# Gate and up of SwiGLU as seven block products for eight, in parts of 8, 8 and 6 tiles

## Chip, core and metric

One Trainium2 chip, one of its cores. The metric is the device time of one execution in microseconds: the median of three runs. All data are float32.

## What is computed

A trunk of four layers on 512 tokens of width 1024. Each layer has a mixer (stick-breaking attention, gMLP, Mamba-2, attention again) and then a SwiGLU FFN with 2816 hidden columns. The change is in the FFN alone:

```python
def swiglu(h, w_gu, w_down):
    gu = h @ w_gu                     # (512, 1024) @ (1024, 5632)
    return (jax.nn.silu(gu[..., :FFN_HIDDEN]) * gu[..., FFN_HIDDEN:]) @ w_down

x = x + swiglu(rmsnorm(x, ffn_norm[i]), ffn_w_gu[i], ffn_w_down[i])
```

## The kernel before

**Layout.** Activations lie transposed: eight tiles `xT[d]` of 128 features by 512 tokens. A float32 product is made from three products of split operands: each operand is a high part (`hi`, a cast to the rounded type fp32r) and a low part (`lo`, the rest), and `mm3` (L420) issues hi*hi, hi*lo and lo*hi. The normed input is kept as `xh[d]` and `xl[d]`, with the norm's gain in it but without the norm's row factor; that factor, `rstdB`, is multiplied in after the product. `xl` is made by a weighted subtraction on VectorE (L570).

**Weights.** `Stream` (L263) brings weights in the order of their use. A piece of 1 MB (1024 x 256 columns) lands in a `raw` tile, of which there are two, by DMAs of SyncE's queue. `_split` (L321) makes the high part on ScalarE or VectorE (`to_hi`, L433 and L435) and the low part on VectorE or GpSimd (`to_lo`, by `either`, L454 and L456), half a piece at a time, 128 x 1024, into rings of three `whi` and three `wlo` tiles.

**The FFN.** `ffn` runs in two parts of 12 and 10 hidden tiles (a tile is 128 columns). For each pair of tiles `fm` (L677) makes gate, then up: two PSUM banks, eight k tiles, 3 matmuls of 512 columns each, 48 matmuls with a piece. A gate's bank is multiplied by `rstdB` (L785), goes through Silu on ScalarE (L788) and once more by `rstdB`; an up's bank is multiplied by that (L802), and the result is split into `hi` and `lo` for the down projection. After a part, `outp` runs its share of the down projection and adds it to `xT` (`residual`, L600). The next sublayer's `xh` and `xl` are made as the last part's residuals come.

**What sets the order.** `Order` (L72) is a planner that runs while the kernel is recorded: it books each operation on its engine with a cost, spawns the chains that follow a matmul, and lets a matmul be recorded when the planned time of what it needs has come. `either`, `to_hi` and `from_psum` choose the engine that is free first in that plan. What it records is the fixed order of each engine's queue; on the chip each queue runs in that order and waits where it must.

## Time and profile before

| what | value |
|---|---|
| median of three runs | 2842.22 us (2841.31 to 2843.84) |
| the profiled execution, its time | 2840.29 us |
| the profiled execution, its span | 2838.6 us |
| TensorE (PE) busy | 2773.0 us, 98% |
| VectorE (DVE) busy | 1837.8 us, 65% |
| ScalarE (ACT) busy | 940.2 us, 33% |
| GpSimd (POOL) busy | 499.5 us, 18% |
| mean granted TensorE clock | 0.993 |

The four FFN stages lie at about 335 to 680, 985 to 1340, 1810 to 2160 and 2480 to 2838 us. PE's matmuls overlap in the trace, since their ends are modelled; the pace of a stream of matmuls is read from its starts. PEld are PE's loads of the stationary operand.

### The profile page before, as it was taken

Reading aid. Unit: us, or ns where it says so; the run is one execution under the profiler, and the core shown is the slowest. Engines: PE = TensorE matmul, PEld = TensorE weight load, DVE = VectorE, ACT = ScalarE, POOL = GpSimd, SP = SyncE. Lnnn points to the kernel's source line nnn. Section 1 sums busy time; section 2 is a strip of 40 time slices with the busy share of each in tenths; the row PEclk is TensorE's granted clock in tenths of the full one; section 3 lists DMA queues with packets and bytes.
Section 4 is the critical chain, followed back from the end, with each engine's and each line's share of the span. In section 5 each row is a group of like instructions: output and inputs, shape, how many; then the busy total and the mean of one; then the engine's idle time right before and its main releaser. Section 6 shows DMA issues by size and latency. Waiting matters only on the chain.

```text
span 2838.6 us, 35548 instructions
## 1 busy us (share of the span) xinstructions
PE 2773.0 (98%) x14531; PEld 2367.4 (83%) x14531; DVE 1837.8 (65%) x2657; ACT 940.2 (33%) x1615; POOL 499.5 (18%) x424
## 2 busy tenths in 40 slices
PE   8999899999999999999999999999999999899999
PEld 8988688888988888888898898788888988688887
DVE  7898754455465655454887797754545899865452
ACT  4777410113322211112453353310112677511111
POOL 4555300002010100001121121100003555300000
PEclk9999999999999999999999999999999999999999
DMA  3110232323332223233222222223222111232222
GB/s 122 60 60 23 82 104 89 102 84 121 99 97 93 89 93 100 89 100 93 77 75 75 81 79 65 89 89 104 89 93 93 54 60 38 68 100 93 93 97 78
DMA packets 212644, 240.77 MB, mean 85 GB/s; under 512 B 6512, under 2 KB 179696, under 8 KB 212480
## 3 DMA queue, kind: packets, MB, share of 16 engines
q1 hardware_dynamic: 212224, 238.36, 26.4%
q8 instruction: 114, 1.87, 0.3%
q14 instruction: 50, 0.41, 0.0%
q0 software_dynamic: 160, 0.11, 0.0%
q10 hardware_dynamic: 96, 0.03, 0.0%
HBM read 236.38 MB, written 2.10 MB: 84 GB/s over the span
## 4 chain that ended last, share of the span: by engine, by line
PE 85%; DVE 12%; ACT 1%; issue 1%; POOL 0%; DMA 0%; ACTq 0%; DVEq 0%; POOLq 0%
PE ps L412 78%; PE c L412 2%; PE z L412 2%; DVE r L454 2%; DVE x L600 1%; DVE xl L570 1%; DVE s L1568 1%; DVE wlo L454 1%; DVE r L435 1%; DVE whi L435 1%; PE t L412 1%; PE c L426 1%; DVE of L1648 0%; DVE s L454 0%; DVE lo L454 0%
## 5 line engine op out<-in xcount | busy, mean ns | idle before, releaser
L412 PE MATMUL ps<-xl,whi 128*128 128x512 f32 x1792 | 700.7, 391 | 4.7 <-DVE xl L570 4.2
L412 PE MATMUL ps<-xh,whi 128*128 128x512 f32 x1792 | 704.2, 393 | 0.0
L412 PE MATMUL ps<-xh,wlo 128*128 128x512 f32 x1792 | 699.1, 390 | 0.0
L454 DVE TENSOR_TENSOR wlo<-raw,whi 128x1024 fp32r<-128x1024 f32 (+2 forms) x413 | 507.7, 1229 | 124.7 <-ACT whi L433 107.1
L433 ACT CAST whi<-raw 128x1024 fp32r<-128x1024 f32 (+2 forms) x235 | 231.0, 983 | 978.9 <-PE ps L412 941.9
L435 DVE CAST whi<-raw 128x1024 fp32r<-128x1024 f32 (+2 forms) x234 | 168.2, 719 | 399.7 <-PE ps L412 399.2
L412 PEld LDWEIGHTS ps<-xl,whi 128*128 128x128 f32 x1792 | 337.5, 188 | 79.6 <-DVE xl L570 9.4
L412 PEld LDWEIGHTS ps<-xh,whi 128*128 128x128 f32 x1792 | 337.5, 188 | 71.3 <-issue 1.4
L412 PEld LDWEIGHTS ps<-xh,wlo 128*128 128x128 f32 x1792 | 337.5, 188 | 70.6
L412 PE MATMUL ps<-hi,wlo 128*128 128x512 f32 x960 | 382.7, 399 | 0.0
L412 PE MATMUL ps<-lo,whi 128*128 128x512 f32 x960 | 379.7, 396 | 0.8 <-DVE lo L454 0.8
L412 PE MATMUL ps<-hi,whi 128*128 128x512 f32 x960 | 380.3, 396 | 0.0
L412 PE MATMUL ps<-whi,xh 128*128 128x256 f32 x1280 | 368.1, 288 | 0.0
L412 PE MATMUL ps<-wlo,xh 128*128 128x256 f32 x1280 | 363.1, 284 | 3.5 <-DVE wlo L454 3.5
L412 PE MATMUL ps<-whi,xl 128*128 128x256 f32 x1280 | 363.0, 284 | 0.0
L412 PEld LDWEIGHTS ps<-wlo,xh 128*128 128x128 f32 x1280 | 245.7, 192 | 5.6 <-DVE wlo L454 3.7
L412 PEld LDWEIGHTS ps<-whi,xh 128*128 128x128 f32 x1280 | 245.7, 192 | 2.3 <-issue 0.2
L412 PEld LDWEIGHTS ps<-whi,xl 128*128 128x128 f32 x1280 | 245.6, 192 | 0.0
L412 PEld LDWEIGHTS ps<-lo,whi 128*128 128x128 f32 x960 | 180.6, 188 | 45.6 <-DVE lo L454 1.5
L412 PEld LDWEIGHTS ps<-hi,whi 128*128 128x128 f32 x960 | 180.7, 188 | 42.3 <-ACT hi L433 0.3
L412 PEld LDWEIGHTS ps<-hi,wlo 128*128 128x128 f32 x960 | 180.8, 188 | 42.2
L456 POOL TENSOR_TENSOR lo<-a,hi 128x512 fp32r<-128x512 f32 x4 | 7.5, 1873 | 1173.8 <-DVE hi L435 1173.8
(232 smaller groups left out, 3435.0 us busy)
## 6 DMA issues: line engine op xcount, KB each, us to landing
raw<-in_ffn_w_gu SPq DMA_DIRECT2D x88, 1024.0 KB, 5.1
raw<-in_ffn_w_down SPq DMA_DIRECT2D x32, 1024.0 KB, 5.1
raw<-in_sb_w_qkv SPq DMA_DIRECT2D x23, 1024.0 KB, 5.2
raw<-in_gm_w_in SPq DMA_DIRECT2D x16, 1024.0 KB, 5.4
raw<-in_ssm_w_in SPq DMA_DIRECT2D x16, 1024.0 KB, 5.5
raw<-in_ffn_w_down SPq DMA_DIRECT2D x16, 768.0 KB, 4.4
raw<-in_gm_w_out SPq DMA_DIRECT2D x8, 1024.0 KB, 5.1
raw<-in_ssm_w_in SPq DMA_DIRECT2D x16, 512.0 KB, 5.3
```

Source lines behind the costliest of these rows:

```text
L412: self.nc.tensor.matmul(out, lhsT=lhsT, rhs=rhs, start=start, stop=stop, skip_group_check=True)
L426: self.nc.tensor.transpose(out, in_, self.ident[:in_.shape[0], :in_.shape[0]])
L433: self.nc.scalar.copy(h, src)
L435: self.nc.vector.tensor_copy(h, src)
L454: self.nc.vector.tensor_tensor(out, a, b, op=op)
L456: self.nc.gpsimd.tensor_tensor(out, a, b, op=op)
L570: nc.vector.scalar_tensor_tensor(out=self.xl[d], in0=x, scalar=gcol(d), in1=self.xh[d].bitcast(F32), op0=ALU.mult, op1=ALU.subtract)
L600: nc.vector.tensor_tensor(self.xT[d], self.xT[d], ps, op=ALU.add)
L1568: nc.vector.scalar_tensor_tensor(out=e, in0=zz, scalar=0.0, in1=e, op0=ALU.max, op1=ALU.add)
```

## The change

Gate and up pieces (all but the first pair of each FFN) go by Strassen's algorithm in Winograd's form. A piece A has 1024 rows by 256 columns, cut into 2 x 2: A11, A12, A21, A22, where the first index is the half of the 256 columns and the second is even or odd k tiles. The input B is cut likewise: even or odd feature tiles, first or second 256 tokens. A piece and the input make a *unit*. With S1 = A21 + A22, S2 = S1 - A11, S3 = A11 - A21, S4 = A12 - S2 and T1 = B12 - B11, T2 = B22 - T1, T3 = B22 - B12, T4 = B21 - T2 (B11, B12 being the token halves of the even tiles) there are seven products: A11 B11, A12 B21, S4 B22, A22 T4, S1 T1, S2 T2, S3 T3. Each is 4 k tiles x 3 matmuls of 256 columns, and the code calls it by the name of its weight factor.

- `halves_in` makes T1 to T4 once per FFN from `xT` and the gains, with differences on ScalarE, VectorE and GpSimd, and splits them into `th` and `tl` tiles of the FFN's pool. No unit starts before all are there; the plain first pair stands ahead of them.
- `_sums` makes S1 to S4 by four operations of 128 x 512 per piece. `_factor` splits each of the seven factors, 512 columns at a time, into one tile that holds high and low part: five of a piece in the `whi` and `wlo` rings (six slots), A22 and S4 in a ring `wt` of two. A third landing tile, `more`, stands beside the two `raw`.
- `fast` orders the products. Three PSUM banks hold a unit's partial sums: X takes A11, S2, S3 and A22 one upon the other, Y takes A12, Z takes S1 and S4. After A11, after S2 and after S3, X is copied out (`saved`, on ScalarE or VectorE), and the next product on X waits for that copy. `added` adds Y or Z to such a copy on VectorE. The last quarter of the result is multiplied straight from X. A unit's A22 and S4 are issued within the next unit; those of a part's last unit stand behind the first piece of the down projection (`between`).
- The parts are 8, 8 and 6 hidden tiles in place of 12 and 10, so `outp` runs three times for each FFN.

```diff
+    def add_fast(self, src):
+        raw = {"srcs": [src], "left": 7, "tag": ("more", "raw", "raw")[self.n_fast % 3], "loaded": Task(), "fast": {}}
+        self.n_fast += 1
+        self.raws.append(raw)
+        for name in ("A11", "A12", "S2", "S1", "S3", "A22", "S4"):
+            p = raw["fast"][name] = {"raw": raw, "task": Task(), "name": name, "slots": 1, "ready": Task()}
+            (self.tails if name in ("A22", "S4") else self.pieces).append(p)
+        return raw["fast"]
...
+    def _sums(self, r):
+        o, fast = self.o, r["fast"]
+        yield r["task"]
+        A = {(i, j): r["ap"][:, j - 1::2, (i - 1) * P:i * P] for i in (1, 2) for j in (1, 2)}
+        fast["A11"]["src"], fast["A12"]["src"], fast["A22"]["src"] = A[1, 1], A[1, 2], A[2, 2]
+        for name in ("A11", "A12", "A22"):
+            o.finish(fast[name]["ready"])
+        new = lambda nm: self.k.fpool.tile([P, 4, P], F32, tag=nm, name="sum", bufs=1)
+        def put(name, dst, a, b, op):
+            yield self.k.either(dst, a, b, op, 512)
+            fast[name]["src"] = dst
+            o.finish(fast[name]["ready"])
+        yield self.k.take("S1", 1)
+        s1 = new("S1")
+        yield from put("S1", s1, A[2, 1], A[2, 2], ALU.add)
+        yield self.k.take("S2", 1)
+        s2 = new("S2")
+        yield from put("S2", s2, s1, A[1, 1], ALU.subtract)
+        yield from put("S3", A[2, 1], A[1, 1], A[2, 1], ALU.subtract)
+        yield fast["A12"]["task"]
+        yield from put("S4", A[1, 2], A[1, 2], s2, ALU.subtract)
+        yield fast["S2"]["task"]
+        self.k.put("S2")
...
+    def _factor(self, p, before, placed, tail=False):
+        if not tail:
+            tag = ("whi", "wlo")[self.turn]
+            self.turn = 1 - self.turn
+        yield p["raw"]["loaded"]
+        yield [p["ready"], before]
+        if tail:
+            t = self.k.fpool.tile([P, 1024], F32R, tag="wt", name="wt", bufs=2)
+        else:
+            t = self.k.wp.tile([P, 1024], F32R, tag=tag, name=tag, bufs=WB)
+        self.o.finish(placed)
+        h, l = (t[:, c:c + 512].rearrange("p (a b) -> p a b", b=P) for c in (0, 512))
+        yield self.k.to_hi(h, p["src"], 512)
+        yield self.k.to_lo(l, p["src"], h, 512, self.slack)
+        p["h"], p["l"] = h, l
+        if p["name"] == "S1":
+            self.k.put("S1")
+        self._done(p)
...
+            b, t12, t34 = (pool.tile([P, S], F32R, tag=f"a{2 + n // 2}{'hl'[n % 2]}", name="t", bufs=1).bitcast(F32)
+                           for n in range(3 * p, 3 * p + 3))
+            T = [t12[:, :H], t12[:, H:], t34[:, :H], t34[:, H:]]
+            nc.scalar.activation(b[:, :H], x0[:, :H], AF.Copy, scale=g0)
+            yield o.A(H, ap=1)
+            stt = lambda out, x, g, y: nc.vector.scalar_tensor_tensor(out=out, in0=x, scalar=g, in1=y,
+                                                                      op0=ALU.mult, op1=ALU.subtract)
+            stt(T[0], x0[:, H:], g0, b[:, :H])
+            yield o.V(H, 1)
+            stt(T[1], x1[:, H:], g1, T[0])
+            yield o.V(H, 1)
+            e = self.either(T[2], T[1], b[:, :H], ALU.subtract, H)
+            stt(T[3], x1[:, :H], g1, T[1])
+            yield [e, o.V(H, 1)]
+            th = self.th[p] = pool.tile([P, 4, H], F32R, name=f"th{p}", bufs=1)
+            tl = self.tl[p] = pool.tile([P, 4, H], F32R, name=f"tl{p}", bufs=1)
+            for n, t in enumerate((t12, t34)):
+                h, l = (q[:, 2 * n:2 * n + 2, :].rearrange("p a b -> p (a b)") for q in (th, tl))
+                yield self.to_hi(h, t, S)
+                e = self.to_lo(l, t, h, S)
+            yield e
+            o.finish(self.t_ready[p])
...
+    def factor_x(self, name, p):
+        H = S // 2
+        if name in ("A11", "A12", "S4"):
+            k, c = {"A11": (0, 0), "A12": (1, 0), "S4": (1, H)}[name]
+            return self.xh[2 * p + k][:, c:c + H], self.xl[2 * p + k][:, c:c + H]
+        n = {"S1": 0, "S2": 1, "S3": 2, "A22": 3}[name]
+        return self.th[p][:, n, :], self.tl[p][:, n, :]
+    def product(self, u, name, bank, start):
+        p = u.p[name]
+        for k in range(4):
+            x, w = self.factor_x(name, k), (p["h"][:, k, :], p["l"][:, k, :])
+            for n, (a, b) in enumerate(((0, 0), (0, 1), (1, 0))):
+                self.nc.tensor.matmul(bank[:, :S // 2], lhsT=w[a], rhs=x[b], start=start and k == 0 and n == 0,
+                                      stop=False, skip_group_check=True)
+                self.o.pe(0.1207)
+        self.stream.release(p)
...
+        def saved(dst, ps, task):
+            if o.pick(A=0.00083 * H + 0.1, V=0.00104 * H + 0.07) == "A":
+                nc.scalar.copy(dst, ps[:, :H])
+                yield o.A(H, True)
+            else:
+                nc.vector.tensor_copy(dst, ps[:, :H])
+                yield o.V(H)
+            o.finish(task)
+        def added(dst, ps, after, task, give):
+            yield after
+            nc.vector.tensor_tensor(dst, ps[:, :H], dst, op=ALU.add)
+            yield o.V(H)
+            if give:
+                self.give()
+            o.finish(task)
+        def p4(u):
+            yield o.due(u.p["A22"]["task"], u.s3)
+            self.product(u, "A22", u.X, False)
+            o.spawn(u.quarter(u.X))
+        def p3(u):
+            yield o.due(u.p["S4"]["task"], u.c22)
+            self.product(u, "S4", u.Z, False)
+            o.spawn(added(u.t[0][:, H:], u.Z, u.s2, u.c12, True))
+        prev = None
+        for u in units:
+            u.s1, u.s2 = Task(), Task()
+            yield self.both(o.due(u.p["A11"]["task"], *self.t_ready), self.bank_cond())
+            u.X = self.bank()
+            self.product(u, "A11", u.X, True)
+            u.t = u.make()
+            o.spawn(saved(u.t[0][:, :H], u.X, u.s1))
+            yield self.both(o.due(u.p["A12"]["task"]), self.bank_cond())
+            u.Y = self.bank()
+            self.product(u, "A12", u.Y, True)
+            o.spawn(added(u.t[0][:, :H], u.Y, u.s1, u.c11, True))
+            o.spawn(u.rest())
+            if prev is not None:
+                yield from p4(prev)
+            yield o.due(u.p["S2"]["task"], u.s1)
+            self.product(u, "S2", u.X, False)
+            o.spawn(saved(u.t[0][:, H:], u.X, u.s2))
+            if prev is not None:
+                yield from p3(prev)
+            yield self.both(o.due(u.p["S1"]["task"]), self.bank_cond())
+            u.Z = self.bank()
+            self.product(u, "S1", u.Z, True)
+            yield o.due(u.p["S3"]["task"], u.s2)
+            self.product(u, "S3", u.X, False)
+            o.spawn(saved(u.t[1][:, H:], u.X, u.s3))
+            o.spawn(added(u.t[1][:, H:], u.Z, u.s3, u.c22, False))
+            prev = u
+        def tail():
+            yield from p4(prev)
+            yield from p3(prev)
+        return tail()
...
+                    yield from between
+                    between = ()
...
-        for nf in (12, 10):
+        for nf in (8, 8, 6):
...
-                gu.append([self.reg_in([wgu[:, :, b + f * P:b + (f + 2) * P]]) for b in (0, HID)])
+                cols = [wgu[:, :, b + f * P:b + (f + 2) * P] for b in (0, HID)]
+                gu.append([self.reg_in([c]) if f == 0 else self.reg_fast(c) for c in cols])
...
+                def quarter(un, by, ready):
+                    def gen(ps):
+                        yield ready
+                        nc.vector.tensor_tensor(un.t[1][:, :H], ps[:, :H], by()[:, :H], op=ALU.mult)
+                        yield o.V(H)
                         self.give()
-                        nc.scalar.activation(gates[i], gates[i], AF.Silu)
-                        yield o.A(S, tab="silu")
-                        yield self.either(gates[i], gates[i], self.rstdB, ALU.mult, S)
-
-                    tasks = {}
-
-                    def gate_(i, ps, tasks=tasks, gate=gate):
-                        tasks[i] = o.spawn(gate(i, ps))
+                        o.finish(un.c21)
+                    return gen
+                def rest(un, by, ready, then):
+                    def first():
+                        yield [un.c11, un.c12, ready[0]]
+                        yield times(un.t[0], slice(0, S), by(0))
+                        yield from then(0)
+                    def second():
+                        yield [un.c22, ready[1]]
+                        e = times(un.t[1], slice(H, S), by(1))
+                        yield [un.c21, e]
+                        yield from then(1)
...
+                def gated(i):
+                    yield from silu(g.t[i])
+                    o.finish(done[i])
+                r = self.rstdB_ready
+                g.quarter = quarter(g, lambda: self.rstdB, r)
+                g.rest = rest(g, lambda i: self.rstdB, [r, r], gated)
+                u.quarter = quarter(u, lambda: g.t[1], done[1])
+                u.rest = rest(u, lambda i: g.t[i], done, lambda i: self.parts(two[i], pool, f"a{n0 + i}", u.t[i]))
+                return [g, u]
```

On **PE**, in the kernel before, the first up block of the first FFN. `ps` is a PSUM bank, the pair behind it is the moving tile and the stationary tile:

```order
L412 MATMUL ps_3969<-xh0_80,whi_3882 128x512
L412 MATMUL ps_3969<-xl0_88,whi_3882 128x512
L412 MATMUL ps_3969<-xh0_80,wlo_3883 128x512
L412 MATMUL ps_3969<-xh1_81,whi_3882 128x512
L412 MATMUL ps_3969<-xl1_89,whi_3882 128x512
L412 MATMUL ps_3969<-xh1_81,wlo_3883 128x512
```

The changed kernel, in the second part of the same FFN: the end of product A12 into bank Y of a unit, then A22 of the unit before it into that one's bank X, and S2 into the current unit's X.

```order
L847 MATMUL ps_5293<-xh7_87,whi_5206 128x256
L847 MATMUL ps_5293<-xl7_95,whi_5206 128x256
L847 MATMUL ps_5293<-xh7_87,whi_5206 128x256
L847 MATMUL ps_5178<-th0_3982,wt_4992 128x256
L847 MATMUL ps_5178<-tl0_3983,wt_4992 128x256
L847 MATMUL ps_5178<-th0_3982,wt_4992 128x256
L847 MATMUL ps_5178<-th3_4068,wt_4992 128x256
L847 MATMUL ps_5272<-th0_3982,wlo_5224 128x256
L847 MATMUL ps_5272<-tl0_3983,wlo_5224 128x256
L847 MATMUL ps_5272<-th0_3982,wlo_5224 128x256
L847 MATMUL ps_5236<-xh1_81,wt_5130 128x256
```

Moving tiles are half as wide, and between A11 and S2 on the same bank stand the 24 matmuls of A12 and of the former unit's A22.

On **DVE**, in the kernel before, most of one gate and one up block in a steady stretch (`g` and `a` are gate and up results):

```order
L785 TENSOR_TENSOR g_4385<-ps_4330,rstdB_3995 128x512
L454 TENSOR_TENSOR g_4385<-g_4385,rstdB_3995 128x512
L785 TENSOR_TENSOR g_4403<-ps_4331,rstdB_3995 128x512
L454 TENSOR_TENSOR wlo_4407<-raw_4310,whi_4406 128x1024
L454 TENSOR_TENSOR g_4403<-g_4403,rstdB_3995 128x512
L435 CAST whi_4436<-raw_4310 128x1024
L454 TENSOR_TENSOR wlo_4437<-raw_4310,whi_4436 128x1024
L802 TENSOR_TENSOR a_4453<-ps_4400,g_4385 128x512
L435 CAST hi_4459<-a_4453 128x512
L454 TENSOR_TENSOR lo_4460<-a_4453,hi_4459 128x512
L802 TENSOR_TENSOR a_4473<-ps_4401,g_4403 128x512
L435 CAST hi_4482<-a_4473 128x512
```

The changed kernel, twelve of the 37 rows that it has for the same two blocks. L870 adds a partial result from PSUM, `sum`, and `raw` or `more` as an output, are S1 to S4, and `wlo`, `whi` and `wt` are low parts written into a factor's tile:

```order
L556 TENSOR_TENSOR sum_5504<-raw_5396 128x512
L556 TENSOR_TENSOR a_5291<-a_5291,g_5198 128x512
L556 TENSOR_TENSOR sum_5516<-sum_5504,raw_5396 128x512
L537 CAST hi_5524<-a_5291 128x512
L556 TENSOR_TENSOR wlo_5521<-more_5208,wlo_5521 128x512
L556 TENSOR_TENSOR lo_5525<-a_5291,hi_5524 128x512
L870 TENSOR_TENSOR g_5423<-ps_5495,g_5423 128x256
L556 TENSOR_TENSOR whi_5545<-raw_5396,whi_5545 128x512
L556 TENSOR_TENSOR g_5423<-g_5423,rstdB_4118 128x256
L556 TENSOR_TENSOR wlo_5566<-raw_5396,wlo_5566 128x512
L870 TENSOR_TENSOR a_5557<-ps_5559,a_5557 128x256
L556 TENSOR_TENSOR raw_5396<-raw_5396,sum_5516 128x4x128
```

Two subtractions of 1024 per piece became seven of 512 and four sums, and the additions from PSUM stand between them in the same queue.

On **DVE** at the start of the first FFN, in the kernel before, from the last residual on:

```order
L600 TENSOR_TENSOR x7_79<-x7_79,ps_3866 128x512
L570 SCALAR_TENSOR_TENSOR xl4_92<-x4_76,cols0_143,xh4_84 128x512
L570 SCALAR_TENSOR_TENSOR xl5_93<-x5_77,cols0_143,xh5_85 128x512
L454 TENSOR_TENSOR wlo_3883<-raw_3763,whi_3882 128x1024
L570 SCALAR_TENSOR_TENSOR xl6_94<-x6_78,cols0_143,xh6_86 128x512
L570 SCALAR_TENSOR_TENSOR xl7_95<-x7_79,cols0_143,xh7_87 128x512
L454 TENSOR_TENSOR acc_3820<-acc_3820,sq_3918 128x512
L454 TENSOR_TENSOR wlo_3928<-raw_3763,whi_3927 128x1024
L643 TENSOR_SCALAR ms_3960<-ps_3953 128x4
L652 TENSOR_SCALAR diag_3958<-ident_96,rstd_3876 128x128 x4
```

The changed kernel, from the last `xl` tile on (the rows go on for 14 more to the last `tl` tile):

```order
L671 SCALAR_TENSOR_TENSOR xl7_95<-x7_79,cols0_143,xh7_87 128x512
L537 CAST wt_3947<-more_3886 128x512
L813 SCALAR_TENSOR_TENSOR t_3927<-x4_76,cols0_143,t_3926 128x256
L813 SCALAR_TENSOR_TENSOR t_3883<-x1_73,cols0_143,t_3882 128x256
L556 TENSOR_TENSOR acc_3820<-acc_3820,sq_3937 128x512
L813 SCALAR_TENSOR_TENSOR t_3909<-x3_75,cols0_143,t_3909 128x256
L556 TENSOR_TENSOR sum_3973<-sum_3949,more_3886 128x512
L556 TENSOR_TENSOR wt_3947<-more_3886,wt_3947 128x512
L813 SCALAR_TENSOR_TENSOR t_3927<-x5_77,cols0_143,t_3927 128x256
L813 SCALAR_TENSOR_TENSOR t_3970<-x6_78,cols0_143,t_3969 128x256
L556 TENSOR_TENSOR acc_3820<-acc_3820,sq_3958 128x512
L813 SCALAR_TENSOR_TENSOR t_3910<-x3_75,cols0_143,t_3909 128x256
```

The differences T (L813) and first factors of the weights stand where two subtractions of weights stood.

## Rows read from the trace of the kernel before

**Rows 1.** The page's busy time (share) and instructions of each engine.

```profile
PE 2773.0 (98%) x14531; PEld 2367.4 (83%) x14531; DVE 1837.8 (65%) x2657; ACT 940.2 (33%) x1615; POOL 499.5 (18%) x424
```

**Rows 2.** Windows: stretch, length, busy PE, PEld, DVE, ACT, POOL; clock, DMA share, GB/s.

```profile
335.00:680.00 345.00, 345.00 (x1502) 282.44 (x1501) 177.92 (x220) 51.70 (x64) 8.26 (x5) 1.00 0.29 92
521.00:532.00 11.00, 11.00 (x50) 9.02 (x49) 4.52 (x6) 1.05 (x1) 0.00 (x0) 1.00 0.28 95
312.00:342.00 30.00, 25.85 (x95) 18.98 (x94) 20.32 (x27) 15.69 (x24) 11.78 (x7) 0.89 0.22 71
100.00:240.00 140.00, 133.88 (x934) 123.66 (x934) 132.40 (x208) 107.62 (x221) 84.72 (x69) 1.00 0.15 51
1460.00:1480.00 20.00, 20.00 (x143) 18.75 (x142) 19.06 (x36) 12.83 (x18) 4.89 (x4) 1.00 0.21 54
```

**Rows 3.** Timeline of PE in gate and up; start, duration, engine, line, operation.

```profile
399.84 0.39 PE L412 MATMUL ps<-xh,whi 128*128 128x512 f32 x1
...
412.53 0.39 PE L412 MATMUL ps<-xh,wlo 128*128 128x512 f32 x1
```

**Rows 4.** Timeline of PE in the first mixer, 256 columns.

```profile
173.88 0.28 PE L412 MATMUL ps<-wlo,xh 128*128 128x256 f32 x1
...
175.55 0.28 PE L412 MATMUL ps<-whi,xh 128*128 128x256 f32 x1
```

**Rows 5.** Timeline of PE in the first FFN's down projection.

```profile
479.62 0.39 PE L412 MATMUL ps<-lo,whi 128*128 128x512 f32 x1
...
483.82 0.39 PE L412 MATMUL ps<-lo,whi 128*128 128x512 f32 x1
```

**Rows 6.** Timeline of DVE behind an up block.

```profile
410.24 0.69 DVE L802 TENSOR_TENSOR a<-ps,g 128x512 f32<-128x512 f32 x1 [0.93 <-PE ps L412]
410.96 0.43 DVE L435 CAST hi<-a 128x512 fp32r<-128x512 f32 x1
411.42 0.69 DVE L454 TENSOR_TENSOR lo<-a,hi 128x512 fp32r<-128x512 f32 x1
```

**Rows 7.** Timeline of DVE in the third mixer.

```profile
1407.20 0.68 DVE L1122 TENSOR_TENSOR xp<-ps,rstdB 128x512 f32<-128x512 f32 x1
1407.80 1.21 DVE L454 TENSOR_TENSOR wlo<-raw,whi 128x1024 fp32r<-128x1024 f32 x1
1408.94 0.74 DVE L1130 SCALAR_TENSOR_TENSOR cv<-xp,cols,cv 128x512 f32<-128x512 f32 x1
1409.60 0.41 DVE L1252 TENSOR_TENSOR h<-h,c 128x256 f32<-128x256 f32 x1
1409.93 0.74 DVE L1130 SCALAR_TENSOR_TENSOR cv<-xp,cols,cv 128x512 f32<-128x512 f32 x1
```

**Rows 8.** Groups of instructions over the whole run: count, busy us, mean ns, idle before.

```profile
L435 DVE CAST whi<-raw 128x1024 fp32r<-128x1024 f32 x213 | 154.0, 723 | 397.6 <-PE ps L412 397.1
...
L435 DVE CAST hi<-a 128x512 fp32r<-128x512 f32 x88 | 37.6, 427 | 3.0
...
L454 DVE TENSOR_TENSOR wlo<-raw,whi 128x768 fp32r<-128x768 f32 x32 | 33.9, 1059 | 88.9 <-ACT whi L433 88.9
...
L1497 DVE SCALAR_TENSOR_TENSOR v<-ps,rstd,v 128x256 fp32r<-128x256 f32 x32 | 15.3, 478 | 8.3 <-ACT v L1495 7.9
...
L1246 ACT COPY h<-c 128x256 f32<-128x256 f32 x8 | 3.0, 370 | 16.7 <-PE c L412 16.7
```

**Rows 9.** The same for DVE between 100 and 240 us.

```profile
L454 DVE TENSOR_TENSOR r<-s,r 128x512 fp32r<-128x512 f32 x28 | 22.8, 816 | 0.8 <-ACT r L433 0.4
L435 DVE CAST r<-s 128x512 fp32r<-128x512 f32 x23 | 15.9, 693 | 0.5 <-ACT s L1611 0.2
...
L454 DVE TENSOR_TENSOR r<-s,r 128x256 fp32r<-128x256 f32 x14 | 9.5, 687 | 0.1
```

**Rows 10.** Timeline of DVE before the first FFN.

```profile
312.41 0.75 DVE L570 SCALAR_TENSOR_TENSOR xl<-x,cols,xh 128x512 fp32r<-128x512 f32 x1 [0.19 <-ACT xh L568]
...
314.28 1.68 DVE L570 SCALAR_TENSOR_TENSOR xl<-x,cols,xh 128x512 fp32r<-128x512 f32 x1
```

173 lines of the change are left out of this document (128 added, 45 removed).

## The prediction

> **What bounds the kernel now.** I read the busy times first [rows 1]: TensorE (PE) holds 98% of the span, VectorE (DVE) 65%, ScalarE (ACT) 33%, GpSimd (POOL) 18%. Then the stretches [rows 2]: in the first SwiGLU stage (335 to 680 us) PE is busy 345.00 of 345 us at granted clock 1.00 and DVE 177.92. A busy PE is a modelled figure, so the pace is taken from starts. In gate and up, matmuls of 512 columns start every 0.2266 us: 56 intervals between the first and the last row of [rows 3]. Nothing else is waited for there; only fewer or shorter matmuls can help, and DVE's spare half is what may be spent.
>
> **PE's share of the change.** A unit is one gate or up block: 1024 rows by 256 weight columns, against 512 tokens. It was 2 x 8 x 3 = 48 matmuls of 512 columns, 48 x 0.2266 = 10.88 us. It becomes 7 products x 4 x 3 = 84 matmuls of 256 columns. Where the kernel before streams 256 columns against a new 128x128 stationary each time, starts are (175.55 - 173.88) / 14 = 0.1193 us apart [rows 4]; 84 x 0.1193 = 10.02 us. The gain is 0.86 us a unit and not an eighth, because a matmul carries about 0.013 us above its columns at either width. There are 20 units in each FFN (the first pair stays plain), 80 in all: **-69 us**. The other end: four of seven products stream from tiles of the FFN's own pool, as the down projection does, and there 512 columns take (483.82 - 479.62) / 18 = 0.2333 us [rows 5]. With that ratio 256 columns cost 0.1228, and the gain is 0.56 x 80 = 45 us. I take 69, since [rows 4] has the shape itself.
>
> **DVE's share.** Per two units DVE had 16 rows; now 37, against 20.0 us of PE: four sums of weight blocks per unit, seven low parts of 512 for two of 1024, three adds of partial results from PSUM, one result multiplied straight from PSUM, and gains on two pieces instead of one. I counted the rows recorded between an FFN part's first product and the first down matmul: for parts one, two and three 62, 86 and 64 two-input operations of 512; 30, 38 and 29 of 256; 9, 12 and 10 casts of 512; two casts and two subtractions of 1024 in parts one and two, four subtractions of 768 in part three. Prices back to back: 0.60 for 512, 1.14 for 1024, 0.33 for 256 (start to start in [rows 7]), cast 0.43 or 0.69 and 1.06 for 768 [rows 8]. That makes 54.7, 73.0 and 56.5 us, together 184.2 for each FFN. At own durations (0.69, 1.22, 0.41 [rows 6, 7]) it is 62.8, 83.9 and 64.6, together 211.3. Which end holds depends on waits: a cast behind the operation that feeds it starts 0.72 us after it and not 0.60 [rows 6]. Many of the new rows feed a near neighbour, so I take the middle: 58.8, 78.5, 60.6.
>
> POOL adds to that. Between 100 and 240 us, with POOL busy 84.72 of 140 us in 69 operations [rows 2], the subtraction of 512 took 816 ns in place of 0.69 us, the cast 693 in place of 427, the subtraction of 256 687 in place of 0.41 us [rows 6 to 9]: 28 x 0.12 + 23 x 0.27 + 14 x 0.28 = 13.5 us, or 0.2 us for each POOL operation. These forms are about a third of DVE's work there and over two thirds in the new phases, so it may be twice that; I take 0.3, on 14, 11 and 7 POOL operations: 4.2, 3.3, 2.1 us. DVE then needs 63.0, 81.8 and 62.7 us.
>
> PE needs 480, 648 and 480 matmuls x 0.1193 = 57.3, 77.3 and 57.3 us. DVE falls behind by 5.7, 4.5 and 5.4 us in a part. What hides lag: bank X takes S2 only after A11 has been copied out of it, and A12 and the former unit's A22 stand between, 24 x 0.1193 = 2.9 us for a PSUM copy of 256 on ACT, 0.37 us [rows 8], and some 0.2 us of hand-over. That leaves 2.3 us. The copies themselves are mostly ACT's, but ACT's queue is in order: a copy stands behind a cast that waits for a sum on DVE, or a Silu that waits for a product on DVE. So DVE's lag reaches PE through ACT. The rest, 3.4 + 2.2 + 3.1 = 8.7 us, is PE idle in each FFN: **+35 us**. As a measure: at 100 to 240 us, where DVE was busy 132.40 of 140, PE was idle 6.1 us, 4.4%; at 1460 to 1480 us, with DVE 19.06 of 20, it was not idle [rows 2]. On 4 x 192 us of the new phases that is 0 to 34 us. The weight tiles themselves are not the tight place (six halves ahead, some seven products or 10 us), nor are the DMAs (the same bytes).
>
> A rule speaks against taking the middle. The Trainium skill, "VectorE: DVE Perf Modes", section "The DRAIN you can't avoid", has the next Vector operation start only once the pipe is empty. By it every operation costs its own duration at the least, DVE's need is the upper end with POOL added, 221 us, the stalls are 22 us in each FFN, and the sum below would give 2877 us. The trace bears it out for chained operations (0.72 us in [rows 6]) and not for unchained ones (0.60 us between starts for 0.68 us of duration in [rows 7]).
>
> **The start of each FFN.** Twelve weighted differences of 256 (T1, T2, T4), four differences (T3) and the splits of eight sums stand on DVE, ACT and POOL; no product starts before all are done. From the last xl row on, 25 DVE rows stand before the last low part: nine weighted differences, eleven of 512, two of 256, two casts, one small. With 0.40 to 0.48 for the first (0.48 is the row in [rows 8], 0.08 less back to back) they sum to 12 to 14 us. Some eight POOL operations run beside them: +2.4 us, and before the change the same neighbours stretched one weighted subtraction from about 0.75 to 1.68 us [rows 10]. PE's cover is the last k of the plain gate and the plain up, 54 x 0.2266 = 12.2 us. It is late by 2 to 6 us; I take 4, so **+16 us** in all. The stretch 312 to 342 us already shows granted clock 0.89 with PE idle 4 us [rows 2]; more idling may cost clock too, which is in the upper end.
>
> **At no cost.** The third part brings 8 more residual adds in each FFN; they fall in down phases, where DVE is busy 4.52 of 11 us [rows 2]. At a part's end the last unit's A22 and S4 stand behind the first down piece, and the second piece, 24 x 0.2333 = 5.6 us, covers the last add, product and split, about 3 us; with DVE late this is the same lag, not another. The mixers keep their order.
>
> **The sum.** -69 + 35 + 16 = -18 us. The profiled execution took 2840.3 us (span 2838.6) and the median is 2842.2; the difference is carried over: 2842 - 18 = **2824 us**.
>
> **Rivals.** (a) *DVE keeps up.* Most rows are unchained, DVE needs 184.2 + 32 x 0.2 = 190.6 us, under PE's 192, and only 0 to 8 us are lost at the starts: 2842 - 69 + 4 = 2777. For it: at 1460 us DVE at 95% cost PE nothing. Against it: no slack remains anywhere.
> (b) *DVE takes over as the bound.* The place is the stretch of products, the chain is sum, cast, low part, evacuation. It decides from 53 us of stalls in the products (69 less 16), 13.3 in each FFN, that is a need of 191.9 + 6.9 + 13.3 = 212 us: only 2% above my 207.5, and just the sum at own durations. With own durations and POOL at 0.42 it is 224.7 us, stalls of 26 x 4 = 104, and the time 2842 - 69 + 104 + 16 = 2893; halfway from the break-even, 2867. For it: every estimate above sits within a tenth of it. Against it: the down phases leave DVE half idle, so lag does not carry from part to part.
> (c) *PE's gain is the small one*, 45 us, because of the new tiles: with my stalls 2842 - 45 + 51 = 2848, no change or a little slower.
>
> **How the numbers follow.** My forecast, 2800 to 2836, has a chance of 0.43; (a) below 2800 0.17; around no change 0.13, most of it (c) or a DVE need near 212; (b) 0.27. A measurement of this kernel can tell about 0.2%, 6 us, so faster means under 2836.5: 0.60; the same 0.13; slower 0.27. The range reaches from 2777 into (b): 2777 to 2876, leaving out about 0.1 on each side.
>
> **What would show it.** In the profile after: starts 0.119 us apart within a product (0.123 would mean (c)); DVE busy over 95% of a part's product stretch; PE idle of some 9 us in each FFN's products, ended by ACT's PSUM copies or by weight halves; some 4 us at each FFN's start, ended by the tl tiles. Products without idle mean (a). If the product stretches of an FFN take over 208 us together, (b) holds. I would be wrong altogether if matmuls of 256 columns slowed while ACT and DVE read PSUM this often, or if PE waited for PSUM banks.

## The result and the profile after

The changed kernel takes 2863.14 us (2861.09 to 2865.79, four runs) against 2841.76 us (2840.42 to 2843.84) for the kernel before on the same chip: a ratio of 1.0075, 95% interval 1.0058 to 1.0093. It is 21 us slower, where 18 us faster was forecast. The time lies inside the range and near rival (b), 2867 us. The profiled spans are 2861.0 and 2838.6 us, so 22.4 us are to be explained.

The page's busy time of after, for [rows 1]:

```profile
PE 2736.2 (96%) x17411; PEld 2465.0 (86%) x17411; DVE 2346.0 (82%) x3682; ACT 1222.9 (43%) x2287; POOL 735.9 (26%) x583
```

TensorE works 37 us less and the kernel still takes longer: TensorE now waits. VectorE is busy 508 us longer, and GpSimd has 159 more operations. The windows of after (columns as in [rows 2]), for the first FFN's start and its three stretches of products:

```profile
316.00:356.00 40.00, 29.86 (x111) 22.14 (x110) 39.97 (x49) 18.04 (x31) 26.94 (x17) 0.87 0.16 53
355.50:429.20 73.70, 69.08 (x530) 66.64 (x529) 70.00 (x111) 30.15 (x59) 20.95 (x14) 0.98 0.30 101
468.50:559.50 91.00, 87.30 (x697) 85.12 (x696) 87.31 (x144) 37.37 (x75) 16.40 (x11) 1.00 0.31 105
598.80:665.30 66.50, 65.08 (x522) 63.69 (x521) 62.81 (x105) 30.33 (x59) 10.19 (x7) 1.00 0.25 84
```

Third number: TensorE busy; fifth: VectorE. In the start VectorE is busy 39.97 of 40 us and TensorE 29.86. In the second part VectorE is busy 96% of the time, TensorE idle for 3.7 us. [rows 2] had TensorE busy 345.00 of 345.

Where the 22.4 us come from follows from the starts of TensorE's matmuls, summed by stage over the four FFNs. Two rows of the table carry everything; the down projections are as before (122.96 to 123.45 us in each FFN, both kernels). The norm's own small matmuls are left out of the second row. "No GpSimd" and "two pairs" are kernels of the experiments below.

| us, sum of four FFNs | before | after | before, no GpSimd | after, no GpSimd | the same, two pairs |
|---|---|---|---|---|---|
| plain pair's first matmul to the next product | 114.7 | 146.7 | 99.5 | 102.1 | 98.0 |
| the other gate and up blocks | 870.6 | 861.2 | 870.6 | 825.1 | 812.0 |
| profiled span | 2838.6 | 2861.0 | 2821.4 | 2781.1 | 2763.7 |

The starts lost 32.0 us and the products gained only 9.4. Without idle time the products run at 0.1196 us a matmul (180.84 us for 1512 in the last kernel of the table), so the 6720 of after would take 803.7 us: a gain of 67 us, of which stalls took back 57.5 (about 3 of these are not waits but matmuls at the lower granted clock, in the first and the fourth FFN).

The waits of TensorE in after, whole run (engine, tile, line, what released it: us in total, times, longest):

```profile
PE ps L847 <- ACT a L861: 27.5, 23, 2.6
...
PE ps L514 <- DVE acc L556: 13.1, 3, 6.3
PE ps L514 <- DVE diag L753: 10.1, 2, 6.1
PE ps L514 <- DVE xl L671: 9.3, 10, 1.6
PE ps L847 <- DVE g L870: 6.1, 6, 1.1
```

L847 is the products, L861 the copy of a bank on ScalarE, L870 the addition of a bank. The others are waits inside the plain pair at the FFN starts, for the norm (`acc`, its sum of squares, and `diag`, its scale) and for `xl`. One of the 23 stalls, in the timeline of TensorE (start, duration, operation, idle time before it):

```profile
504.35 0.27 PE L847 MATMUL ps<-th,whi 128*128 128x256 f32 x1
505.85 0.39 PE L847 MATMUL ps<-th,wlo 128*128 128x256 f32 x1 [1.22 <-ACT a L861]
```

and ScalarE's timeline there:

```profile
504.90 0.63 ACT L1013 ACTIVATE g<-g 128x512 f32<-128x512 f32 x1 [3.95 <-DVE g L1051]
505.44 0.35 ACT L861 COPY a<-ps 128x256 f32<-128x256 f32 x1
```

ScalarE stood 3.95 us at a Silu that waited for VectorE, with the copy of bank X behind it, and TensorE waited for the copy. This is the path that the prediction described.

What VectorE does at such a place, in its timeline:

```profile
506.35 0.69 DVE L556 TENSOR_TENSOR wlo<-sum,wlo 128x512 fp32r<-128x512 f32 x1
506.95 0.42 DVE L870 TENSOR_TENSOR g<-ps,g 128x256 f32<-128x256 f32 x1
507.29 1.47 DVE L556 TENSOR_TENSOR sum<-raw 128x512 f32<-128x512 f32 x1
508.68 0.68 DVE L556 TENSOR_TENSOR g<-g,rstdB 128x512 f32<-128x512 f32 x1
509.28 0.68 DVE L556 TENSOR_TENSOR sum<-sum,raw 128x512 f32<-128x512 f32 x1
509.89 0.68 DVE L556 TENSOR_TENSOR whi<-raw,whi 128x512 fp32r<-128x512 f32 x1
510.49 1.78 DVE L556 TENSOR_TENSOR raw<-raw 128x512 f32<-128x512 f32 x1
512.20 0.41 DVE L870 TENSOR_TENSOR a<-ps,a 128x256 f32<-128x256 f32 x1
```

and GpSimd's timeline of the same microseconds:

```profile
506.91 1.30 POOL L558 TENSOR_TENSOR wt<-more,wt 128x512 fp32r<-128x512 f32 x1 [7.87 <-ACT wt L535]
510.11 1.62 POOL L558 TENSOR_TENSOR g<-g,rstdB 128x512 f32<-128x512 f32 x1 [1.89 <-ACT g L1013]
```

VectorE runs without a gap, 0.60 us from start to start, except where a GpSimd operation runs. GpSimd's at 506.91 ends at 508.21; VectorE's `sum<-raw`, begun at 507.29, ends at 508.76, 0.55 after that. GpSimd's at 510.11 ends at 511.73; `raw<-raw` ends at 512.27, 0.54 after. So the VectorE operation seems to stand still until GpSimd is through. The one that reads a bank, at 506.95, keeps its 0.42 us. A stretched operation loses 0.8 to 1.1 us, more than the 0.60 us that the same work takes on VectorE itself.

**Theory:** GpSimd's operations are what makes VectorE late, in the products and at the starts. **Rivals:** the third part of each FFN, the hand-over of banks through ScalarE's queue, or simply too many operations for VectorE. A fourth, that somebody waits for the results of the slower GpSimd, finds little in the waits of after: those that a GpSimd operation ended come to 5.7 us for TensorE in the whole run, none of them in the products.

### The profile page after: what moved, and what is told of

The parts are those of the page before. It is cut to its first block, busy times and chain, and to the rows that moved or that the text cites. A ratio compares the mean times of both kernels' runs of the same rounds, so it can differ in the third digit from the quotient of the medians.

```text
span 2861.0 us, 43572 instructions
## 1 busy us (share of the span) xinstructions
PE 2736.2 (96%) x17411; PEld 2465.0 (86%) x17411; DVE 2346.0 (82%) x3682; ACT 1222.9 (43%) x2287; POOL 735.9 (26%) x583
## 4 chain that ended last, share of the span: by engine, by line
PE 60%; DVE 32%; issue 4%; ACT 3%; DMA 1%; POOL 0%; ACTq 0%; DVEq 0%; POOLq 0%
PE ps L514 45%; PE ps L847 9%; DVE wlo L556 3%; PE c L514 2%; DVE sum L556 2%; PE z L514 2%; DVE raw L556 2%; DVE r L556 2%; DVE whi L556 2%; DVE lo L556 2%; DVE xl L671 1%; DVE x L701 1%; DVE t L813 1%; DVE whi L537 1%; DVE s L1861 1%
## 5 line engine op out<-in xcount | busy, mean ns | idle before, releaser
L535 ACT CAST whi<-raw 128x1024 fp32r<-128x1024 f32 (+2 forms) x207 | 177.1, 856 | 384.8 <-PE ps L514 351.5
L556 DVE TENSOR_TENSOR wlo<-raw,whi 128x1024 fp32r<-128x1024 f32 (+2 forms) x251 | 304.4, 1214 | 37.2 <-ACT whi L535 28.2
L701 DVE TENSOR_TENSOR x<-x,ps 128x512 f32<-128x512 f32 x232 | 157.5, 684 | 125.2 <-PE ps L514 124.5
L537 DVE CAST whi<-raw 128x1024 fp32r<-128x1024 f32 (+1 forms) x181 | 124.4, 687 | 142.3 <-PE ps L514 126.6
L847 PE MATMUL ps<-th,wlo 128*128 128x256 f32 x960 | 194.4, 284 | 23.9 <-ACT a L861 22.4
L514 PE MATMUL ps<-xl,whi 128*128 128x512 f32 x512 | 204.7, 400 | 9.4 <-DVE xl L671 9.3
L514 PE MATMUL ps<-xh,whi 128*128 128x512 f32 x512 | 208.3, 407 | 0.0
L514 PE MATMUL ps<-xh,wlo 128*128 128x512 f32 x512 | 203.1, 397 | 0.0
L847 PE MATMUL ps<-th,whi 128*128 128x256 f32 x960 | 194.2, 284 | 0.7 <-ACT g L861 0.7
L558 POOL TENSOR_TENSOR g<-g,rstdB 128x512 f32<-128x512 f32 (+1 forms) x37 | 55.1, 1488 | 532.0 <-DVE g L870 317.4
```

What stands on the lines that cost most here:

```text
L514: self.nc.tensor.matmul(out, lhsT=lhsT, rhs=rhs, start=start, stop=stop, skip_group_check=True)
L535: self.nc.scalar.copy(h, src)
L537: self.nc.vector.tensor_copy(h, src)
L556: self.nc.vector.tensor_tensor(out, a, b, op=op)
L558: self.nc.gpsimd.tensor_tensor(out, a, b, op=op)
L701: nc.vector.tensor_tensor(self.xT[d], self.xT[d], ps, op=ALU.add)
```

## The experiments

**The parts alone.** The kernel before, with this edit:

```diff
-        for nf in (12, 10):
+        for nf in (8, 8, 6):
-                o.run(self.outp(down, ys, half == 1))
+                o.run(self.outp(down, ys, half == 2))
```

> The kernel before with the hidden axis of each FFN cut into parts of 8, 8 and 6 tiles in place of 12 and 10; no block products. The theory (the 21 us that the change cost come from VectorE: 8 us more at each FFN start and 14 us of stalls inside each FFN's products) gives no change here: 2842 us, within 4. The rival, that a third part itself costs (one more down projection's start and end in each of four FFNs, some 2 to 4 us each), gives 2850 to 2858.

Measured: 2842.11 us, ratio 1.0006 (0.9996 to 1.0015). The third part costs nothing, as was said under "At no cost"; with the block products in it, it was not tried by itself.

**No sums of weight blocks.** In `_sums` the four operations go, and the factors read raw blocks:

```diff
-        yield from put("S1", s1, A[2, 1], A[2, 2], ALU.add)
...
+        for name, ij in (("S1", (2, 1)), ("S2", (1, 1)), ("S3", (2, 1)), ("S4", (1, 2))):
+            fast[name]["src"] = A[ij]
```

> The changed kernel without the four sums over weight blocks (S1 to S4): the factors are split straight from raw blocks. It leaves that part of the computation out. Eighty units lose 4 elementwise operations each, 2.4 us of VectorE per unit at 0.60 us each, or what their GpSimd shares cost VectorE. If VectorE's lag is what stalls the products, most of their 55 us of stalls goes and the start of each FFN gets some microseconds shorter too: 2863 less 50 to 65, 2800 to 2813. The rival, that the stalls are the hand-over of PSUM copies from one bank's use to the next and have nothing to do with how much VectorE has to do, gives 2855 to 2863.

Measured: 2800.32 us, ratio 0.9859 (0.9845 to 0.9874). The products take 807.5 us, hardly above the 803.7 without stalls. The hand-over of banks, which is all still there, therefore costs nothing when VectorE keeps up. It doesn't yet single out GpSimd, because the planner then also gave it less: the page's busy line of this kernel, then the window of its second part.

```profile
PE 2712.5 (97%) x17411; PEld 2453.7 (88%) x17411; DVE 2190.5 (78%) x3631; ACT 1151.8 (41%) x2134; POOL 560.8 (20%) x467
```

```profile
460.00:550.00 90.00, 90.00 (x710) 87.91 (x709) 80.02 (x151) 29.83 (x59) 0.00 (x0) 1.00 0.35 118
```

116 fewer GpSimd operations than in after, none in this stretch, and TensorE busy 90.00 of 90.

**No preparation of the activations.** `halves_in` isn't called, and `factor_x` returns halves of `xh` and `xl` for all seven products:

```diff
-            self.halves_in(pool, gcol)
+            self.t_ready = []
```

> The changed kernel without the sums over blocks of the activations and their splits: the products stream halves of the plain x instead. It leaves that part of the computation out. Theory: the 32 us that the four FFN starts lost are this work's, so 2863 less 28 to 34, 2829 to 2835, with the stalls inside the products as they were. The rival, that the start is late because the first unit's weight blocks are not there yet, gives 2855 to 2863.

Measured: 2824.93 us, ratio 0.9946 (0.9931 to 0.9961), 38 us less than after and 4 beyond the range expected. The starts fall to 121.5 us, within 7 of the kernel before, so 25 of the 32 us are this work's, with what its GpSimd operations cost (the kernel has 541 of them for 583). The other 13 come from the products (847.7 us), probably because they begin without a VectorE that is already late; that was not shown by itself.

**No GpSimd in the FFNs.** Only the choice of the engine changes, between the opening of the FFN's pool and its end:

```diff
     def either(self, out, a, b, op, n, slack=0.0):
-        if o.pick(V=0.00104 * n + 0.07 + slack, G=0.0021 * n + 0.15) == "V":
+        if self.fpool is not None or o.pick(V=0.00104 * n + 0.07 + slack, G=0.0021 * n + 0.15) == "V":
```

> The changed kernel with every elementwise operation of the FFNs that the planner could give to GpSimd kept on VectorE. Theory: beside each GpSimd operation VectorE lost 0.8 to 1.1 us, more than the 0.6 us that the operation takes on VectorE itself, so with some 32 of them per FFN and more at the starts the kernel gets 20 to 70 us faster: 2793 to 2843. The rival, that GpSimd relieves VectorE after all, as the prediction's 0.3 us for each had it, gives 32 x 0.3 us more in each FFN and more than that at the starts: 2875 to 2940.

Measured: 2782.80 us (2782.59 to 2783.44), ratio 0.9798 (0.9783 to 0.9813). The sign is the theory's and the size beyond its range: 80 us faster than after and 58 faster than the kernel before. The page's busy line, then the second part's window, then VectorE's timeline in it:

```profile
PE 2707.2 (97%) x17411; PEld 2452.8 (88%) x17411; DVE 2249.4 (81%) x3795; ACT 1283.3 (46%) x2367; POOL 454.9 (16%) x390
```

```profile
455.00:546.00 91.00, 91.00 (x719) 88.91 (x718) 85.55 (x157) 42.21 (x81) 0.00 (x0) 1.00 0.36 117
```

```profile
491.21 0.68 DVE L556 TENSOR_TENSOR sum<-raw 128x512 f32<-128x512 f32 x1
491.81 0.68 DVE L556 TENSOR_TENSOR g<-g,rstdB 128x512 f32<-128x512 f32 x1
492.42 0.68 DVE L556 TENSOR_TENSOR wt<-more,wt 128x512 fp32r<-128x512 f32 x1
493.02 0.69 DVE L556 TENSOR_TENSOR sum<-sum,raw 128x512 f32<-128x512 f32 x1
```

193 operations left GpSimd. VectorE runs 113 more than in after (the planner moved 80 casts and copies on to ScalarE, which has room) and is busy 97 us less. So each GpSimd operation had cost VectorE about (96.6 + 113 x 0.60) / 193 = 0.85 us, taking 0.60 for each that it now runs more. Counted by kinds it is some 0.9: the 193 that VectorE took over (171 of 512 columns, 19 of 256, 3 of 1024) are 112 us back to back, and the 80 that it gave away were casts of some 37 us in all, so (96.6 + 112 - 37) / 193. One GpSimd operation stays in each FFN start, the norm's `rstd` (L748), which is not among those that the planner places. VectorE at 94% in the second part holds TensorE up nowhere.

**The kernel before without GpSimd in its FFNs**, by the same edit of `either`:

> The kernel before (no block products) with the elementwise operations of its four FFNs kept off GpSimd. The run without GpSimd in the changed kernel started its FFNs 12.6 us quicker in sum than the kernel before does (102.1 us from the first matmul of the plain pair to the next product, against 114.7). Theory: that part is owed to GpSimd's operations and not to the block products, so this gives 2826 to 2834, and of the 58 us by which the changed kernel without GpSimd beats the kernel before, some 45 to 50 are the block products' own. Rival: with VectorE at 65% the kernel before does not feel its GpSimd operations at all, 2838 to 2845.

Measured: 2823.89 us, ratio 0.9933 (0.9913 to 0.9954), a little below the theory's range. Nearly all of it is at the starts (99.5 us for 114.7, 15.2 of the 17.2 us between the spans); the products keep 870.6 us to the digit. So the block products alone, without GpSimd on either side, are worth 2823.9 - 2782.8 = 41 us.

**A Silu that waits for nothing.** To try the path through ScalarE's queue, in the units of the changed kernel:

```diff
-                nc.scalar.activation(g, g, AF.Silu)
+                nc.scalar.activation(pool.tile([P, S], F32, tag="free", name="free", bufs=1),
+                                     self.rstdB, AF.Silu)
```

> The changed kernel with the units' Silu reading a tile that is long there and writing a scratch tile, so that it waits for no VectorE operation and ScalarE's queue holds no copy of a bank behind it. It leaves the Silu of the 20 units' gates per side out of the computation. If the lag of VectorE reaches TensorE only through ScalarE's queue, the stalls of some 1.4 us before S2 and S3 go, and most of the 55 us of stalls with them: 2820 to 2835. The rival: VectorE itself has too little time in the products (96% busy in the second part), so the stalls move to the products that wait for its additions and factors: 2850 to 2860.

Measured: 2857.04 us, 6 us less than after (ratio to before 1.0049, 1.0036 to 1.0062). The rival holds. TensorE's waits, whole run:

```profile
PE ps L847 <- DVE g L870: 11.2, 8, 2.0
...
PE ps L847 <- DVE a L870: 10.0, 15, 2.0
...
PE ps L847 <- ACT g L861: 9.1, 10, 1.5
```

Of the 27.5 us behind `ACT a L861` 0.5 are left, and 21.2 us of waits for VectorE's additions stand in their place (6.1 in after). Behind `ACT g L861` it is 9.1 us for 3.8, so ScalarE's queue was not freed altogether. It was the way by which most of the lag reached TensorE, not its cause.

**One extra operation per unit, on GpSimd or on VectorE**, in the changed kernel without GpSimd; for VectorE `nc.vector` and `o.V(S)`:

```diff
+        def extra():
+            t = self.fpool.tile([P, S], F32, tag="extra", name="extra", bufs=1)
+            nc.gpsimd.tensor_tensor(t, self.rstdB, self.rstdB, op=ALU.mult)
+            yield o.G(S)
...
             self.product(u, "S1", u.Z, True)
+            o.spawn(extra())
```

> The changed kernel without GpSimd in its FFNs (2782.8 us), with one extra GpSimd operation per unit, 512 columns, two inputs in SBUF, into a scratch tile that nobody reads: 80 in all, nobody waits for them. The theory, that each costs VectorE 0.8 to 1.1 us while it runs, gives VectorE, which is 97% busy in the products, 64 to 88 us more, of which it has some 20 us to spare: 2825 to 2855. The price in the prediction, 0.3 us each, gives 24 us, most of it in VectorE's spare time: 2783 to 2793.

> The same with the extra operation on VectorE in place of GpSimd. At 0.60 us start to start, 80 of them are 48 us, of which VectorE has some 20 us to spare: 2803 to 2820, less than the same operation costs on GpSimd. The rival, that an operation is cheaper for the kernel on GpSimd than on VectorE, as the planner's prices have it, puts this run above the one with the extra GpSimd operation.

Measured: 2831.67 us with the 80 on GpSimd, 2786.10 us with them on VectorE. The first is as the theory had it: 48.9 us, 0.61 us each, though nobody reads what they write, and though VectorE and ScalarE run the same 3795 and 2367 operations as without. The second is cheaper than I expected, 3.3 us, hardly more than the spread of its runs (2782.36 to 2787.49); the planner moved 24 casts to ScalarE, and VectorE is busy only 28.3 us more.

The two do not stand at the same places. VectorE's extra operations lie among the units, but GpSimd's queue waited for `rstdB` alone and then ran its 20 of an FFN one behind another in some 28 us, at the start of the products. All of the loss is there: in the second FFN the first part's products take 69.60 us for 57.83, and the second and third part's 77.52 and 57.43 us in both kernels. So the two runs show that GpSimd operations alone make TensorE wait, but give no ratio of prices. GpSimd's timeline (eight operations in a line), then VectorE's there:

```profile
1002.12 10.90 POOL L888 TENSOR_TENSOR extra<-rstdB 128x512 f32<-128x512 f32 x8
```

```profile
1003.63 1.52 DVE L556 TENSOR_TENSOR more<-more 128x512 f32<-128x512 f32 x1
1005.08 1.52 DVE L556 TENSOR_TENSOR whi<-more,whi 128x512 fp32r<-128x512 f32 x1
1006.52 0.41 DVE L870 TENSOR_TENSOR g<-ps,g 128x256 f32<-128x256 f32 x1
1006.86 0.41 DVE L864 COPY g<-ps 128x256 f32<-128x256 f32 x1
1007.19 0.59 DVE L537 CAST whi<-sum 128x512 fp32r<-128x512 f32 x1
1007.70 1.52 DVE L556 TENSOR_TENSOR g<-g,rstdB 128x512 f32<-128x512 f32 x1
1009.15 1.53 DVE L556 TENSOR_TENSOR wlo<-sum,wlo 128x512 fp32r<-128x512 f32 x1
```

This is the mechanism by itself: in these lines every VectorE operation with two inputs in SBUF takes 1.45 us from start to start for 0.60, 0.85 more; operations of the two engines alternate. Those that read a bank keep 0.41 us, so not every GpSimd operation meets one that it stretches: in the mean of the 80 VectorE is busy 0.64 us longer for each (2300.7 us for 2249.4). The window of that stretch against the same 30.9 us without the extra operations (first with, then without):

```profile
999.10:1030.00 30.90, 22.84 (x182) 21.77 (x180) 30.90 (x35) 11.62 (x23) 26.95 (x20) 1.00 0.11 36
```

```profile
985.40:1016.30 30.90, 30.90 (x257) 30.66 (x256) 30.90 (x59) 20.08 (x39) 0.00 (x0) 1.00 0.29 92
```

VectorE is busy throughout in both, with 35 operations in one and 59 in the other; a busy share does not tell work from waiting.

**The same beside plain products.** In the kernel before without GpSimd, two such operations for each pair of hidden tiles but a part's first:

> The kernel before without GpSimd in its FFNs (2823.9 us), with two extra GpSimd operations of 512 columns per pair of hidden tiles into a scratch tile that nobody reads: 72 in all, placed as in the run with one per unit, which cost 49 us for 80. Theory: they cost VectorE their 0.8 to 1.1 us here too, but VectorE has a third of its time free beside plain products, so the time does not move: 2822 to 2828. Rival: a GpSimd operation in the products holds TensorE up whatever VectorE has to do: at 0.6 us each 43 us, 2860 to 2870.

Measured: 2826.11 us, against 2823.9 without; every FFN stage has the same length within 0.02 us. Two windows of the first FFN, with the extra operations and without:

```profile
341.70:370.00 28.30, 28.30 (x126) 23.46 (x125) 26.73 (x25) 6.49 (x9) 24.26 (x18) 1.00 0.27 88
```

```profile
341.70:370.00 28.30, 28.30 (x126) 23.44 (x125) 18.66 (x26) 5.44 (x7) 0.00 (x0) 1.00 0.24 76
```

VectorE is busy 8 us longer for 18 operations, 0.45 each and not the 0.8 to 1.1 that was expected, and TensorE does not notice. In the products GpSimd's price is paid only where VectorE has no time to spare, which is why the kernel before could live with it there; at its FFN starts it paid 15 us.

**Towards a better kernel.** Two plain pairs at each FFN's start, GpSimd off everywhere, and both:

```diff
-                gu.append([self.reg_in([c]) if f == 0 else self.reg_fast(c) for c in cols])
+                gu.append([self.reg_in([c]) if f in (0, 2) else self.reg_fast(c) for c in cols])
-                    if n == 0 and not ys:
-                        plain(g_pieces, u_pieces, two)
+                    if n == 0 and len(ys) < 4:
+                        plain(g_pieces, u_pieces, two, len(ys))
```

> The changed kernel without GpSimd in its FFNs (2782.8 us), with two plain pairs at each FFN's start in place of one, so that 16 units per FFN's sides are left to the block products. In two of the four FFNs of that run TensorE stood some 7 us behind the row norm's scale and then ran its first products at the lower clock, 9 us lost in each beside the other two. If the second pair covers the preparation, that gain of up to 18 us stands against 8 more plain tile products at 0.86 us each, 7 us: 2770 to 2778. The rival: the wait is the norm's own chain, which no longer start hides, and only the 7 us remain: 2786 to 2793.

> The changed kernel with every two-input elementwise operation that the planner chooses an engine for on VectorE, in the mixers too. Theory: an operation on GpSimd costs VectorE more than it takes on VectorE itself wherever VectorE sets the pace, and nothing elsewhere; the mixers' starts have it waiting in places: 2765 to 2783. Rival: in the mixers TensorE waits for chains in which GpSimd works beside VectorE, which get longer on one engine: 2785 to 2800.

> Both of the last two together. Theory: the two touch different places, so their differences from 2782.8 add up; 2755 to 2780. Rival: two plain pairs only matter while GpSimd works at the starts, then it is the run without GpSimd anywhere, within 4 us.

Measured: 2765.54 us (2765.45 to 2767.88), 2833.05 us and 2813.25 us. The first is the best kernel here: ratio to before 0.9730 (0.9716 to 0.9745). It is 17 us better than one plain pair, more than was expected, and its products (18 units in each FFN, not 16) have no stall left. With one pair, the first FFN's start shows why (timelines of TensorE and of GpSimd in the changed kernel without GpSimd, then the window around it):

```profile
350.48 2.07 PE L514 MATMUL ps<-diag,ones 128*128 128x512 f32 x2 [6.85 <-DVE diag L753]
...
353.21 0.41 PE L847 MATMUL ps<-tl,whi 128*128 128x256 f32 x1
353.42 0.41 PE L847 MATMUL ps<-th,whi 128*128 128x256 f32 x1
```

```profile
345.71 3.81 POOL L748 TENSOR_TENSOR rstd<-ms,mhalf 128x4 f32<-128x4 f32 x1 [27.43 <-DVE ms L744]
```

```profile
340.50:355.00 14.50, 7.65 (x43) 6.41 (x43) 13.04 (x27) 4.27 (x9) 3.81 (x1) 0.76 0.23 72
```

TensorE stood 6.85 us behind the norm's scale, and 3.81 us of them are the one operation that was left on GpSimd; after that matmuls start 0.21 us apart and not 0.12, and the window's granted clock is 0.76 (it is granted 2.4 GHz for part of the time and 1.2 for the rest). The second pair puts work over the gap.

GpSimd off everywhere (113 operations that the planner does not place stay on it) was missed by both sides of the expectation: 50 us slower than off in the FFNs alone. The differences add up (2782.8 - 17.3 + 50.3 = 2815.8, measured 2813.25), so this is another place: the FFNs begin later, 333.5 us for 314.9 in the first layer. TensorE's waits in the whole run, first for GpSimd off everywhere, then for off in the FFNs:

```profile
PE z L514 <- DVE r L556: 33.5, 33, 2.4
PE z L514 <- ACT r L535: 14.1, 10, 1.8
PE c L528 <- DVE y L1603: 11.0, 2, 5.6
```

```profile
PE z L514 <- DVE r L556: 15.2, 17, 1.8
...
PE c L528 <- DVE y L1603: 3.8, 1, 3.8
```

In the mixers GpSimd shortens chains for which TensorE waits, and what it costs there is less than what it brings. Why the two places differ beyond that was not tried further.

## Why the prediction was wrong

Its sum was -69 + 35 + 16 = -18 us; measured are -67 + 57.5 + 32.0 = +22.5. Of the 40 us between them 22.5 lie in the stalls of the products, 16 at the starts and 2 in TensorE's pace.

- **TensorE's term was right.** 67 us against 69: the products run at 0.1196 us a matmul in the kernel without stalls, for the 0.1193 of [rows 4]. Rival (c), 0.1228, is out.
- **"I take 0.3": the price of a GpSimd operation beside VectorE is the step that failed.** It was drawn from mean durations in the first mixer [rows 9], a mixture of VectorE operations that were stretched and many that were not: 24 of the 28 subtractions of 512 there took 0.67 to 0.69 us, the other four 1.20 to 2.73. An operation with two inputs in SBUF that meets a GpSimd one of 512 columns loses 0.85 us. The row that showed it was at hand: [rows 10], 1.68 us for 0.75. The count, 32 in the products of an FFN, was right (14 + 11 + 7 in the windows above). With 0.85 and the step's own back-to-back sum, VectorE's need is 184.2 + 32 x 0.85 = 211.4 us; less 192 for TensorE and 6.9 of lead, 12.5 us are lost in each FFN, 50 in all, against 57.5 measured; with the 0.9 of the run without GpSimd it is 56. By parts the stalls are 26.1, 21.6 and 9.9 us over the four FFNs, in the order of those counts.
- **The middle between the two VectorE prices was the wrong choice too, the other way.** The back-to-back end holds: 0.60 from start to start in after and in the kernel without GpSimd. Two errors in opposite directions left 207.5 us near the 211 that the right prices give, which is why the forecast stood so close to its break-even of 212. (A cast of 1024 is 0.72 us in [rows 8] and not 0.69, which moves the sums by 0.1.)
- **The start of an FFN was taken at 4 us and took 8**, above the upper bound of 6. The operations were counted and priced as if GpSimd took some of them off VectorE for 0.3 us each.
- **The place of the wait at the start was wrong too.** It was to be ended by the `tl` tiles, just ahead of the products, and no wait of TensorE in after is for one. TensorE waits earlier, inside the plain pair, for the norm's `acc` and `diag` and for `xl` (32.5 us; waits for the same three come to 12.3 in the kernel before), which come late from a VectorE that also makes T1 to T4; this is at a granted clock of 0.87 in the window from 316 to 356 us (0.89 in the like one of [rows 2]).
- **What of this goes with GpSimd.** Without GpSimd the starts take 102.1 us, 12.6 less than in the kernel before and 2.6 more than there without GpSimd. But in two FFNs of that kernel the wait for the norm's scale has moved right behind the start, among the products, where it costs 18 us that the second plain pair took back. Counted with them, about 11 of the 32 us go with GpSimd at the starts, and of the 57.5 in the products about 54 (825.1 - 803.7 leaves 21, 18 of them this wait).
- **The path was right and its weight was not.** The lag reached TensorE through ScalarE's queue, as was said (27.5 us of waits), but taking that path away gave back 6 us of 57.5. Whoever TensorE waits for is not thereby the cause.
- **Rival (b) came true in its place and its size, not for its reason.** It needed 53 us of stalls, and there were 57.5. It blamed VectorE operations at own durations; they ran faster than that. Its own sign, product stretches of an FFN over 208 us together, was met in one FFN of four (207.6, 204.1, 205.0 and 210.3 us).
- **Rival (a) did not hold for the kernel as changed, but nearly did as soon as GpSimd was out**: it gave 2777 us, and the kernel without GpSimd takes 2782.8, of which the two places with the waiting norm and the lower clock are 18. What it needed was 190.6 us of VectorE time; I had argued that no slack remained anywhere, and did not ask what the kernel would do if GpSimd's share went back.

On the rule that was weighed there: by the Trainium skill, "VectorE: DVE Perf Modes", section "The DRAIN you can't avoid", the next Vector operation starts only when the pipe is empty, except that one which is not held back starts earlier. The prediction left the exception out, and the timelines above are of that kind: 0.60 us between starts of operations of 0.68 us, wherever GpSimd is quiet. So the time that the rule gave, 2877 us, is near the measured one by luck.

The rule that I passed over stands in the Trainium skill, "SBUF — State Buffer", sections "Who interferes with whom" and "Summary: rules for kernel authors": a VectorE instruction with two SBUF inputs contends with a GpSimd instruction that reads SBUF, and the second to issue is blocked until the first is through. The trace agrees: 1.52 us instead of 0.68 beside a chain of GpSimd operations, and 0.41 us unchanged for those that read a bank.

## What to carry to other kernels

Before an elementwise operation is put on GpSimd to relieve VectorE, price it by what it does to the neighbours: two inputs in SBUF on both sides cost VectorE 0.85 us here for 0.60 of work taken over. It cost nothing where VectorE had time to spare, and it paid in the mixers, where it shortens a chain that TensorE waits for. When a change moves work onto an engine that others lean on, make its price from single rows in which the two meet, not from a mean. And when a queue's head is seen to hold up the bound engine, ask whether the work behind it would have come any sooner; a run that frees the head tells.

## What was not expected of the hardware

- VectorE and GpSimd alternate whole operations: the eight GpSimd operations in 10.90 us come 1.36 us apart in the mean, and where one VectorE operation of two SBUF inputs follows another between them, those start 1.45 us apart.
- It is not only operations with two inputs. At the start of the first FFN in after, a cast on VectorE took 2.62 us, ending 0.28 us after a GpSimd subtraction of 1024 columns (331.27 + 2.84 = 334.11; the cast's mean is 0.43 in [rows 8]). The two rows, of VectorE and of GpSimd:

```profile
331.77 2.62 DVE L537 CAST wt<-more 128x512 fp32r<-128x512 f32 x1
```

```profile
331.27 2.84 POOL L558 TENSOR_TENSOR wlo<-raw,whi 128x1024 fp32r<-128x1024 f32 x1
```

- VectorE counts as busy while it stands: 30.90 of 30.90 us with 35 operations or with 59.
